# Feature-first copies of x, memory and norms, and one pinned order for the first loads

## The chip, the cores and the metric

The kernel runs on one NeuronCore of a Trainium2 chip. A core has five engines with an instruction stream each: TensorE (PE, matmuls and transposes; PEld is its weight load, which overlaps), VectorE (DVE), ScalarE (ACT), GpSimd (POOL) and SyncE (SP, here only the issuer of loads). Each works in the order in which its instructions stand and waits on semaphores. Sixteen DMA engines carry out the transfers that SP, ACT and POOL issue. The metric is the time of one execution in microseconds, lower is better. The kernel before took 2638.45 us, the median of three timed runs.

## The reference

Four layers on a sequence of 256 tokens of width 2048, in float32. Every layer norms x, makes one combined input projection, runs a mixer (latent attention, sparse attention, sliding window, latent attention), adds four heads of cross-attention to a memory of 256 tokens, gates the lot and projects it back:

```
mem_n = rmsnorm(mem, mem_norm)
for i in range(4):
    h = rmsnorm(x, norm_in[i])
    self_out, mq, gate = mixer(h, w_in)          # by layer: MLA, DSA, SWA, MLA
    mem_out = memory_attention(mq, mem_n @ w_mem_kv[i])
    y = concat(self_out, mem_out) * silu(gate)
    x = x + y @ w_out[i]
return rmsnorm(x, final_norm)
```

For this change two facts matter. A product `rmsnorm(m, g) @ w` contracts over the 2048 features, so TensorE wants the features of m on the partitions, each multiplied by its g; the factor 1/rms of a row can be applied to the result. And all four `mem_n @ w_mem_kv[i]` depend on memory alone.

## The kernel before, in words

Precision first: a float32 operand is split into a high and a low part (`split`: ACT copies the high part to the fast matmul type at L60, DVE subtracts it at L64), and a product is three matmuls, high by high, high by low and low by high. Every weight therefore passes through ACT (`wh`) and DVE (`wl`), three buffers each, after its load into one of five buffers `wr` of 512 KB (`stage`, L207, on SP's queue).

`rows_by` (L234 to L236) computes a 256 x 512 product with tokens as rows: per k-tile of 128 features six matmuls, and two k-tiles per load. `columns_by` (L253, L257) computes one with features as rows, in the same way.

The program begins with `memory()`. It loads memory in rows, in four tiles `mrow` of 512 features, on SP's and ACT's queues; loads the norm weights as rows and transposes them into `gvec` (`vectors_T`, L91); transposes each memory tile with TensorE, multiplies it by its norm weights and splits it (`to_features`, L186 to L188); and sums the squares of the rows on ACT (`square_sum`, L197) for 1/rms, `mrstd` by rows and `mbc` spread over columns. The result `mT` feeds eight equal steps (two for each layer): a `rows_by` product for two heads' values, `acc_mv`, scaled by `mrstd` as it leaves PSUM, and two `columns_by` products for two heads' keys, `acc_mk`, scaled by `mbc`. POOL writes them to HBM (`mv`, `mkT`) for later.

Within the first step stand also `late_constants` (x by rows in four loads of 512 KB at L115, three norm vectors, masks, rotary tables) and, at its end, the same transposing and splitting for x (`Norm.chunk`, into `xT`) with its sums and 1/rms (`Norm.finish`), and the bias tables (`bias_table`, `pt` at L142). After each step one table copy of 1.5 MB goes out on POOL's queue (`tab<-flat`, L151), after the second step two. `mrow`, the keys on their way out and later tiles share five buffers, `pq`.

The order on each engine is set by a scheduler that moves instructions by modelled times; only what is passed through `keep_in_program_order` keeps its place. Loads of SP and ACT share eight semaphores in turn, so at most eight are in flight, and one more waits for the landing of an older one.

Of the kernel before, what the change touches and what calls it, by code (L numbers as in the profile page):

```python
# [8 lines left out]
F32 = mybir.dt.float32  # L9
# [22 lines left out]
def kernel(ctx: ExitStack, tc: tile.TileContext, a: dict, out: bass.AP,  # L32
# [10 lines left out]
    def misc(name, dt=F32):  # L43
        return ps.tile([P, 512], dt, name=name, tag="mp", bufs=4)
# [27 lines left out]
    rows = cst.tile([P, P], F32, name="rows")  # L72
    mrow = []

    def vectors(src, o, n, eng):
        if len(src.shape) == 2:
            src = src.rearrange("l d -> (l d)")
        eng.dma_start(rows[o:o + n, :], src.rearrange("(r c) -> r c", c=P))

    def memory_rows(c):  # L80
        q = act.tile([P, 2, 512], F32, name="mrow", tag="pq", bufs=PQ)
        mrow.append(q)
        for t in range(2):
            eng = nc.scalar if t else nc.sync
            eng.dma_start(q[:, t, :], min_[t][:, c * 512:(c + 1) * 512])

    gvec = cst.tile([P, P], F32, name="gvec")

    def vectors_T(o, n):
        gp = misc("gp")  # L90
        nc.tensor.transpose(gp[:, :n], rows[o:o + n, :], ident[o:o + n, o:o + n])  # L91
        nc.vector.tensor_copy(gvec[:, o:o + n], gp[:, :n])
# [9 lines left out]
    nc.vector.tensor_copy(identr, ident)  # L102
    ones = cst.tile([P, P], F32, name="ones")
    nc.vector.memset(ones, 1.0)

# [2 lines left out]
    sin = cst.tile([P, 2, A_ROPE], F32, name="sin")  # L108
    nsink = cst.tile([P, 32], F32, name="nsink")

    def late_constants():
        for c in range(2):
            for t in range(2):
# [13 lines left out]
        nc.vector.tensor_scalar(nsink, nsink, -1.0, None, op0=OP.mult)  # L127
# [54 lines left out]
    def to_features(dst, t, src, gcol, n=4):  # L182

        tp = misc("tp")
        for j in range(n):
            nc.tensor.transpose(tp[:, j * P:(j + 1) * P], src[:, j * P:(j + 1) * P], ident)  # L186
        xg = tmp("xg")
        nc.vector.tensor_mul(xg[:, :n * P].rearrange("p (j c) -> p j c", j=n),  # L188
                             tp[:, :n * P].rearrange("p (j c) -> p j c", j=n),
                             gvec[:, gcol:gcol + n][:, :, None].to_broadcast([P, n, P]))  # L190
        sl = slice(t * P, (t + 1) * P)
        g3 = xg[:, :n * P].rearrange("p (j c) -> p j c", j=n)
        split(dst[:, 0, :n, sl], dst[:, 1, :n, sl], g3)

    def square_sum(col, src):
        junk = tmp("junk")
        nc.scalar.activation(junk[:, :src.shape[-1]], src, AF.Square, accum_out=col)  # L197
# [21 lines left out]
        split(wh[:, :n], wl[:, :n], wr[:, c0:c0 + n])  # L219
        return wh, wl  # L220

    def rows_by(xt, kts, w, k0, cols, name):

        acc = [ps.tile([P, 512], F32, name=f"acc_{name}{t}", tag="acc", bufs=4) for t in range(2)]
        for s in range(0, kts, ST):
            m = min(ST, kts - s)
            wr, n = stage(w, k0 + s, m, cols)
            for k in range(m):
                wh, wl = parts_of(wr, k * n, n)
                q = xt[(s + k) // 4]  # L230
                for t in range(2):
                    xh, xl = (q[:, v, (s + k) % 4, t * P:(t + 1) * P] for v in range(2))
                    first, last = s + k == 0, s + k == kts - 1
                    nc.tensor.matmul(acc[t][:, :n], xh, wh[:, :n], start=first, stop=False)  # L234
                    nc.tensor.matmul(acc[t][:, :n], xh, wl[:, :n], start=False, stop=False)  # L235
                    nc.tensor.matmul(acc[t][:, :n], xl, wh[:, :n], start=False, stop=last)  # L236
        return acc
# [38 lines left out]
    class Norm:  # L276
# [32 lines left out]
    def memory():  # L309
        mrstd = cst.tile([P, 2], F32, name="mrstd")  # L310
        m16 = cst.tile([P, 2], F32, name="m16")
        mbc = act.tile([P, S], F32, name="mbc", tag="kr", bufs=1)
        mss = small("mss", 8, bufs=2)
        mT = []
        for c in range(4):
            if c < 2:
                memory_rows(c + 2)
            q = act.tile([P, 2, 4, S], F32R, name="mT", tag=f"big{c}")
            mT.append(q)
            for t in range(2):  # L320
                to_features(q, t, mrow[c][:, t, :], c * 4)
                square_sum(mss[:, t * 4 + c:t * 4 + c + 1], mrow[c][:, t, :])
        s2 = small("ms2", 2)
        nc.vector.tensor_reduce(s2, mss.rearrange("p (t c) -> p t c", t=2), AX.X, OP.add)
        rsqrt_mean(mrstd, s2, D)
        nc.vector.tensor_scalar(m16, mrstd, 0.0625, None, op0=OP.mult)
        spread(mbc, m16)
        copies = [(v, g) for v in range(2) for g in range(4)]
        for i in range(depth):
            w = a["w_mem_kv"][i]  # L330
            for p_ in range(2):
                acc = rows_by(mT, 16, w, 0, (MEMW + p_ * 512, 512), "mv")
                v = [act.tile([P, 2, 512], F32R, name="mv", tag="aux", bufs=AUX) for z in range(2)]
                for t in range(2):
                    sc = mrstd[:, t:t + 1]
                    copy_act(v[0][:, t, :], acc[t], scale=sc)
                    nc.vector.scalar_tensor_tensor(v[1][:, t, :], acc[t], sc, f32(v[0])[:, t, :],
                                                   op0=OP.mult, op1=OP.subtract)
                for z in range(2):
                    nc.gpsimd.dma_start(mv[i][p_][:, z], v[z])  # L340
                if i == p_ == 0:
                    late_constants()
                for h in (2 * p_, 2 * p_ + 1):
                    acc = columns_by(mT, 16, w, 0, (h * 256, 256), "mk")
                    kT = act.tile([P, 2, 2, S], F32R, name="mkT", tag="pq", bufs=PQ)
                    for j in range(2):
                        z = total(acc[j])
                        zs = wk.tile([P, S], F32, name="zs", tag="z", bufs=3)
                        nc.vector.tensor_mul(zs, z, mbc)
                        split(kT[:, 0, j, :], kT[:, 1, j, :], zs)  # L350
                    nc.gpsimd.dma_start(mkT[i][h], kT)
                step = 2 * i + p_
                if step == 0:
                    for c in range(4):
# [500 lines left out]
def _constants():  # L855
# [18 lines left out]
            "c_cos": np.concatenate([c, c], 1), "c_sin": np.concatenate([-s, s], 1)}  # L874


_INS = ["x", "mem", "norm_in", "final_norm", "mem_norm", "rel_bias", "w_in_a", "a_q_norm", "w_uq",
        "a_kv_norm", "w_ukv", "w_in_b", "w_in_c", "c_sinks", "w_mem_kv", "w_out"]


# [19 lines left out]
```

## Time and profile before

| | |
|---|---|
| timed runs | 2636.72, 2638.45, 2638.67 us (median 2638.45) |
| profiled execution | 2637.23 us, span 2635.0 us |
| busy | PE 2605.1 us (99%), DVE 1890.2 (72%), ACT 1625.5 (62%), POOL 57.8 (2%) |
| first matmul of the first product | 13.84 us after the span's start |
| memory's eight steps | until about 376 us |
| moved by DMA | 507.50 MB, mean 193 GB/s; 262 to 290 GB/s in the first 400 us |

A row of the timeline gives start and duration in us, engine, line, operation, tiles, shape and count, and in brackets the idle time before it with its cause. A row of windows gives the stretch and its length, then busy time (and instructions) of PE, PEld, DVE, ACT and POOL, the granted TensorE clock, the share of the DMA engines and GB/s; restricted to a tile, engines without such instructions are left out. A row of DMA issues ends with the median time from issue to landing. A row of groups gives the total and mean (ns) time and the idle time in front. A row of the chain gives start, duration and what it was. A row of waits gives total, times and longest.

### The profile page before, as it was taken

How to read it: one execution, taken by the hardware profiler on the slowest of the kernel's cores; microseconds unless marked ns; L12 is line 12 of the kernel's file. 1: busy time of each engine (PE TensorE's matmuls, PEld its weight loads, DVE VectorE, ACT ScalarE, POOL GpSimd, SP SyncE). 2: the span in 40 equal slices, each digit the busy share in tenths (PEclk: the TensorE clock that was granted, in tenths of full speed). 3: DMA queues.
4: the chain of work that ended last, by engine and by line, in shares of the span. 5: the costliest groups of instructions: out<-in, count | busy, mean ns of one | idle time of the engine just before them, and what ended most of it. 6: DMA issues, size and time to landing. Idle time of an engine off the chain costs nothing.

```text
span 2635.0 us, 43048 instructions
## 1 busy us (share of the span) xinstructions
PE 2605.1 (99%) x14623; PEld 2260.1 (86%) x14623; DVE 1890.2 (72%) x4174; ACT 1625.5 (62%) x3460; POOL 57.8 (2%) x102
## 2 busy tenths in 40 slices
PE   8999999999999999999999999999999999999998
PEld 7888888888888889888888888888888888888886
DVE  7566656677767685877777776777778767776767
ACT  6455556556656566666666666676666655665655
POOL 1000000000000000000000000000000000000000
PEclk9999999999999999999999999999999999999999
DMA  7898886666557666565556665555555766665764
GB/s 268 272 290 275 273 265 199 165 187 168 169 160 224 192 189 171 167 183 170 175 164 190 188 191 176 173 172 177 191 168 162 206 163 188 165 171 156 226 183 135
DMA packets 454064, 507.50 MB, mean 193 GB/s; under 512 B 69300, under 2 KB 352180, under 8 KB 452692
## 3 DMA queue, kind: packets, MB, share of 16 engines
q1 hardware_dynamic: 439716, 446.42, 57.3%
q0 software_dynamic: 13120, 56.17, 6.7%
q8 instruction: 115, 1.88, 0.3%
q10 hardware_dynamic: 1008, 2.16, 0.2%
q14 instruction: 105, 0.86, 0.1%
HBM read 485.70 MB, written 31.56 MB: 196 GB/s over the span
## 4 chain that ended last, share of the span: by engine, by line
PE 97%; DMA 1%; DVE 1%; ACT 0%; issue 0%; ACTq 0%; POOLq 0%
PE acc_g L253 14%; PE acc_g L257 7%; PE acc_wo L234 7%; PE acc_wo L235 7%; PE acc_wo L236 7%; PE acc_mq L253 5%; PE acc_mk L253 5%; PE acc_qn L253 3%; PE acc_cq L253 3%; PE acc_mq L257 2%; PE acc_mk L257 2%; PE acc_q L234 2%; PE acc_q L235 2%; PE acc_q L236 2%; PE acc_mv L235 2%; PE acc_mv L236 2%
## 5 line engine op out<-in xcount | busy, mean ns | idle before, releaser
L64 DVE TENSOR_TENSOR wl<-wr,wh 128x512 fp32r<-128x512 f32 (+2 forms) x1776 | 1172.9, 663 | 642.9 <-ACT wh L60 612.7
L60 ACT ACTIVATE wh<-wr 128x512 fp32r<-128x512 f32 (+2 forms) x1776 | 1079.9, 609 | 846.1 <-PE acc_g L253 186.0
L253 PE MATMUL acc_g<-xT,wh 128*128 128x512 f32 x1536 | 488.9, 397 | 0.6 <-DVE z L264 0.6
L257 PEld LDWEIGHTS acc_g<-xT,wl 128*128 128x128 f32 x1536 | 285.2, 188 | 60.7
L257 PE MATMUL acc_g<-xT,wl 128*128 128x256 f32 x1536 | 311.0, 280 | 0.0
L235 PE MATMUL acc_wo<-wl,y 128*128 128x512 f32 x768 | 302.5, 394 | 0.6 <-DVE wl L64 0.5
L236 PE MATMUL acc_wo<-wh,y 128*128 128x512 f32 x768 | 299.1, 390 | 0.0
L253 PEld LDWEIGHTS acc_g<-xT,wh 128*128 128x128 f32 x1536 | 238.1, 189 | 4.7 <-issue 1.1
L234 PE MATMUL acc_wo<-wh,y 128*128 128x512 f32 x768 | 240.4, 393 | 0.7 <-ACT wh L60 0.6
L235 PEld LDWEIGHTS acc_wo<-wl,y 128*128 128x128 f32 x768 | 144.3, 188 | 30.0 <-DVE wl L64 1.4
L236 PEld LDWEIGHTS acc_wo<-wh,y 128*128 128x128 f32 x768 | 144.2, 188 | 28.4
L234 PEld LDWEIGHTS acc_wo<-wh,y 128*128 128x128 f32 x768 | 141.3, 188 | 27.8 <-ACT wh L60 1.0
L253 PE MATMUL acc_mk<-mT,wh 128*128 128x512 f32 x512 | 160.8, 396 | 1.4 <-ACT wh L60 1.4
L253 PE MATMUL acc_mq<-xT,wh 128*128 128x512 f32 x512 | 161.7, 397 | 0.0
L807 DVE TENSOR_TENSOR x<-x,acc_wo 128x512 f32<-128x512 f32 x192 | 125.5, 681 | 7.2 <-PE acc_wo L236 6.9
L253 PE MATMUL acc_qn<-cT,wh 128*128 128x512 f32 x384 | 123.2, 399 | 0.0
L253 PE MATMUL acc_cq<-xT,wh 128*128 128x512 f32 x384 | 120.8, 396 | 0.0
L257 PEld LDWEIGHTS acc_mk<-mT,wl 128*128 128x128 f32 x512 | 95.8, 188 | 22.7 <-DVE wl L64 0.4
L257 PEld LDWEIGHTS acc_mq<-xT,wl 128*128 128x128 f32 x512 | 93.7, 188 | 20.0
L257 PE MATMUL acc_mq<-xT,wl 128*128 128x256 f32 x512 | 102.5, 281 | 0.0
L235 PE MATMUL acc_q<-wl,xT 128*128 128x512 f32 x256 | 102.4, 400 | 0.0
L257 PE MATMUL acc_mk<-mT,wl 128*128 128x256 f32 x512 | 100.8, 278 | 0.0
(284 smaller groups left out, 4453.5 us busy)
## 6 DMA issues: line engine op xcount, KB each, us to landing
wr<-in_w_out_dram SPq DMA_DIRECT2D x192, 512.0 KB, 3.7
wr<-in_w_in_a_dram SPq DMA_DIRECT2D x176, 512.0 KB, 4.2
wr<-in_w_mem_kv_dram SPq DMA_DIRECT2D x128, 512.0 KB, 5.2
wr<-in_w_in_b_dram SPq DMA_DIRECT2D x112, 512.0 KB, 3.7
wr<-in_w_in_c_dram SPq DMA_DIRECT2D x104, 512.0 KB, 3.7
wr<-in_w_uq_dram SPq DMA_DIRECT2D x288, 128.0 KB, 2.8
tab<-flat POOLq DMA_DIRECT2D x8, 1536.0 KB, 10.9
wr<-in_w_in_a_dram SPq DMA_DIRECT2D x32, 288.0 KB, 3.0
```

Source lines behind the costliest of these rows:

```text
L60: nc.scalar.activation(o, i, AF.Copy, scale=scale)
L64: nc.vector.tensor_sub(lo, src, f32(hi))
L234: nc.tensor.matmul(acc[t][:, :n], xh, wh[:, :n], start=first, stop=False)
L235: nc.tensor.matmul(acc[t][:, :n], xh, wl[:, :n], start=False, stop=False)
L236: nc.tensor.matmul(acc[t][:, :n], xl, wh[:, :n], start=False, stop=last)
L253: nc.tensor.matmul(acc[j], wh[:, o:o + P], q[:, :, kt % 4, :], start=kt == 0, stop=False)
L257: nc.tensor.matmul(acc[j][:, 0, :], wl[:, o:o + P], q[:, 0, kt % 4, :], start=False, stop=kt == kts - 1)
L807: nc.vector.tensor_add(xs, xs, acc[t])
```

## The change

x, memory and the norm weights come in a second layout, features on partitions (`l_x`, `l_mem`: 128 x 16 x 256; `l_norms`: all weights as columns of one 128 x 128 tile), made before the launch. `gvec` is loaded whole. A tile `ft` of features is multiplied and split straight from its load, in parts 256 wide: ACT writes the high part with the norm weight as scale, DVE the low one (`weighted_parts`). The transposes of memory, of x for layer 0 and of the norm rows go; those of x between layers stay.

All loads of the first step go on SP's queue in one pinned order: norms, first features, and then features between weights. Memory and x are still read by rows as well, for the sums of squares and the residual: memory's rows behind the first product's weights, x's rows behind the weights of steps 2 to 5 (steps counted from 0), a quarter each. A quarter of x's features follows each, and `finish` moves to step 6. The first values leave PSUM after the first key head, behind the row scales.

```diff
+    gvec = cst.tile([P, P], F32, name="gvec")
+    tc.keep_in_program_order(nc.sync.dma_start(gvec, a["l_norms"]))
+
+    def features(src, c):
+        q = act.tile([P, 4, S], F32, name="ft", tag="pq", bufs=PQ)
+        for k in range(0, 4, 2):
+            tc.keep_in_program_order(
+                nc.sync.dma_start(q[:, k:k + 2, :], src[:, 4 * c + k:4 * c + k + 2, :]))
+        return q
+
+    mft = [features(a["l_mem"], 0)]
     ident = cst.tile([P, P], F32, name="ident")
-    nc.scalar.dma_start(ident, a["c_ident"])
...
-    memory_rows(0)
-    vectors(a["mem_norm"], 0, 16, nc.gpsimd)
-    memory_rows(1)
-    vectors_T(0, 16)
...
+    def first_rows(c):
+        for t in range(2):
+            cs = slice(c * 512, (c + 1) * 512)
+            tc.keep_in_program_order(nc.sync.dma_start(x[t][:, cs], xin[t][:, cs]))
+
     def late_constants():
-        for c in range(2):
-            for t in range(2):
-                cs = slice(c * 1024, (c + 1) * 1024)
-                nc.sync.dma_start(x[t][:, cs], xin[t][:, cs])
-        vectors(a["norm_in"], 64, 64, nc.sync)
-        vectors(a["a_q_norm"], 32, 24, nc.sync)
-        vectors(a["a_kv_norm"], 56, 8, nc.sync)
-        vectors_T(64, 64)
-        vectors_T(32, 32)
...
+    def weighted_parts(dst, src, gcol):
+        for k in range(4):
+            g = gvec[:, gcol + k:gcol + k + 1]
+            copy_act(dst[:, 0, k, :], src[:, k, :], scale=g)
+            nc.vector.scalar_tensor_tensor(dst[:, 1, k, :], src[:, k, :], g, f32(dst)[:, 0, k, :],
+                                           op0=OP.mult, op1=OP.subtract)
...
-    def rows_by(xt, kts, w, k0, cols, name):
+    def rows_by(xt, kts, w, k0, cols, name, prepare=None):
...
             wr, n = stage(w, k0 + s, m, cols)
+            if prepare is not None and s % 4 == 0:
+                prepare(s // 4)
...
+            if self.layer == 0:
+                weighted_parts(q, features(a["l_x"], c), 64 + c * 4)
             for t in range(2):
                 src = x[t][:, c * 512:(c + 1) * 512]
-                to_features(q, t, src, 64 + self.layer * 16 + c * 4)
+                if self.layer:
+                    to_features(q, t, src, 64 + self.layer * 16 + c * 4)
                 square_sum(self.ss[:, t * 4 + c:t * 4 + c + 1], src)
...
+        def prepare(c):
+            if c < 3:
+                mft.append(features(a["l_mem"], c + 1))
+            if c == 1:
+                tc.keep_in_program_order(nc.sync.dma_start(ident, a["c_ident"]))
+                nc.vector.tensor_copy(identr, ident)
+            weighted_parts(mT[c], mft[c], c * 4)
...
+                begins = i == p_ == 0
+                acc = rows_by(mT, 16, w, 0, (MEMW + p_ * 512, 512), "mv", prepare if begins else None)
+                if begins:
+                    mrow = [memory_rows(c) for c in range(4)]
+                else:
+                    values(i, p_, acc)
+                for h in (2 * p_, 2 * p_ + 1):
+                    acck = columns_by(mT, 16, w, 0, (h * 256, 256), "mk")
+                    if begins and h == 0:
+                        row_scales(mrow)
+                        values(i, p_, acc)
+                    keys(i, h, acck)
+                if begins:
                     late_constants()
...
                 if step == 0:
-                    for c in range(4):
-                        nm.chunk(c)
-                    nm.finish()
                     bias_table(0)
                     bias_table(1)
+                if 2 <= step < 6:
+                    first_rows(step - 2)
+                    nm.chunk(step - 2)
+                if step == 6:
+                    nm.finish()
```

`values`, `keys` and `row_scales` hold the code that stood in the loop and ahead of it before.

More of the change, by code (lines that the diff above doesn't have):

```diff
@@ L101 @@
     identr = cst.tile([P, P], F32R, name="identr")
-    nc.vector.tensor_copy(identr, ident)
     ones = cst.tile([P, P], F32, name="ones")
@@ L313, in memory @@
         mss = small("mss", 8, bufs=2)
-        mT = []
-        for c in range(4):
[L316 to L319, printed above, removed]
-            for t in range(2):
[L321 to L324, printed above, removed]
@@ L325, in memory @@
-        rsqrt_mean(mrstd, s2, D)
-        nc.vector.tensor_scalar(m16, mrstd, 0.0625, None, op0=OP.mult)
-        spread(mbc, m16)
+        mT = [act.tile([P, 2, 4, S], F32R, name="mT", tag=f"big{c}") for c in range(4)]
+        def prepare(c):
[5 more added lines that the diff above has]
+            weighted_parts(mT[c], mft[c], c * 4)
@@ new lines, in memory_rows, with row_scales @@
+        def memory_rows(c):
+            q = act.tile([P, 2, 512], F32, name="mrow", tag="pq", bufs=PQ)
+            for t in range(2):
+                tc.keep_in_program_order(
+                    nc.sync.dma_start(q[:, t, :], min_[t][:, c * 512:(c + 1) * 512]))
+            return q
+        def row_scales(mrow):
+            for c in range(4):
+                for t in range(2):
+                    square_sum(mss[:, t * 4 + c:t * 4 + c + 1], mrow[c][:, t, :])
+            s2 = small("ms2", 2)
+            nc.vector.tensor_reduce(s2, mss.rearrange("p (t c) -> p t c", t=2), AX.X, OP.add)
+            rsqrt_mean(mrstd, s2, D)
+            nc.vector.tensor_scalar(m16, mrstd, 0.0625, None, op0=OP.mult)
+            spread(mbc, m16)
@@ new lines, in values @@
+        def values(i, p_, acc):
+            v = [act.tile([P, 2, 512], F32R, name="mv", tag="aux", bufs=AUX) for z in range(2)]
+            for t in range(2):
+                sc = mrstd[:, t:t + 1]
+                copy_act(v[0][:, t, :], acc[t], scale=sc)
+                nc.vector.scalar_tensor_tensor(v[1][:, t, :], acc[t], sc, f32(v[0])[:, t, :],
+                                               op0=OP.mult, op1=OP.subtract)
+            for z in range(2):
+                nc.gpsimd.dma_start(mv[i][p_][:, z], v[z])
@@ L328, in memory, with keys @@
+        def keys(i, h, acc):
+            kT = act.tile([P, 2, 2, S], F32R, name="mkT", tag="pq", bufs=PQ)
+            for j in range(2):
+                z = total(acc[j])
+                zs = wk.tile([P, S], F32, name="zs", tag="z", bufs=3)
+                nc.vector.tensor_mul(zs, z, mbc)
+                split(kT[:, 0, j, :], kT[:, 1, j, :], zs)
+            nc.gpsimd.dma_start(mkT[i][h], kT)
         copies = [(v, g) for v in range(2) for g in range(4)]
@@ L889 @@
     arrays, args = {}, {}
-    for name, v in [(n, inputs[n]) for n in _INS] + list(_constants().items()):
+    for name, v in ([(n, inputs[n]) for n in _INS] + list(_laid_out(inputs).items())
+                    + list(_constants().items())):
         v = _np.ascontiguousarray(v)
```

50 lines of the change are left out of this document (11 added, 39 removed).

## The prediction

> **What bounds the kernel now.** I read the page's busy shares first, then the first microseconds instruction by instruction, then TensorE's waits, then stretches by window, then the loads' times to landing.
>
> ```profile
> span 2635.0 us, 43048 instructions
> PE 2605.1 (99%) x14623; PEld 2260.1 (86%) x14623; DVE 1890.2 (72%) x4174; ACT 1625.5 (62%) x3460; POOL 57.8 (2%) x102
> ...
> PE gp L91 <- DMA rows<-in_mem_norm_dram: 7.2, 1, 7.2
> PE acc_kvb L234 <- ACT wh L60: 1.8, 1, 1.8
> PE acc_mk L253 <- ACT wh L60: 1.4, 1, 1.4
> ...
> 200.00:250.00 50.00, 50.00 (x253) 42.39 (x252) 32.07 (x56) 27.49 (x50) 3.46 (x7) 1.00 0.84 264
> ```
>
> PE is busy 99% of the span, and 50.00 of 50 us in a stretch of the memory stage. It waits 7.2 us for the first load and hardly at all later. So whatever leaves PE's order shortens the time, and whatever makes PE wait lengthens it. Nothing else counts. The start, row by row:
>
> ```profile
> 7.15 0.28 PE L91 MATMUL gp<-ident,rows 16*128 16x16 f32 x1 [7.15 <-DMA rows<-in_mem_norm_dram]
> 7.37 4.71 PE L186 MATMUL tp<-ident,mrow 128*128 128x128 f32 x28
> 13.84 0.73 PE L234 MATMUL acc_mv<-wh,mT 128*128 128x512 f32 x2 [0.67 <-ACT wh L60]
> 15.73 0.42 PEld L234 LDWEIGHTS acc_mv<-wh,mT 128*128 128x128 f32 x2
> 22.67 0.41 PEld L234 LDWEIGHTS acc_mv<-wh,mT 128*128 128x128 f32 x2
> 25.39 0.41 PEld L234 LDWEIGHTS acc_mv<-wh,mT 128*128 128x128 f32 x2
> ...
> 35.39 1.09 PE tp L186 x10
> ```
>
> The real matmuls begin at 13.84. One k-tile of `rows_by` (six matmuls) takes 1.36 us (22.67 to 25.39 is two). The second k-tile begins at 15.73, so the stream runs as if it had begun at 15.73 - 1.36 = 14.37 us. Ten transposes of x take 1.09 us, 0.109 each.
>
> **The change, part by part.** The built order of PE is the old one without 67 instructions: 32 transposes of memory, 32 of x, 3 of the norm rows. A few `spr` and `pt` matmuls stand elsewhere; the rest keeps its order to the end.
>
> *Transposes of x and norms.* The 32 of x lie inside packed PE time (the first step): 32 x 0.109 = -3.5 us. Of the three `gp`, two lie there, about 0.15 each: -0.3.
>
> *The start.* The new order on SP's queue is norms (64 KB), first memory features (512 KB), first weights (512 KB), features, two weights, features, `ident`, two weights, features, weights. No POOL load is in the way any more. What moved in the first microseconds (last column, GB/s), and two landings:
>
> ```profile
> 0.00:2.00 2.00, 0.00 (x0) 0.00 (x0) 0.23 (x2) 0.00 (x0) 0.93 (x6) 1.00 0.11 14
> 2.00:4.00 2.00, 0.00 (x0) 0.00 (x0) 0.00 (x0) 1.49 (x2) 0.42 (x1) 1.00 0.84 235
> 4.00:6.00 2.00, 0.00 (x0) 0.00 (x0) 0.23 (x1) 0.72 (x2) 0.00 (x0) 1.00 0.75 214
> 6.00:8.00 2.00, 0.85 (x4) 0.81 (x5) 0.17 (x1) 0.00 (x0) 0.00 (x0) 1.00 1.02 382
> 8.00:10.00 2.00, 2.00 (x12) 2.00 (x11) 1.32 (x3) 0.76 (x2) 0.00 (x0) 1.00 1.02 367
> 12.00:14.00 2.00, 0.89 (x6) 0.58 (x6) 2.00 (x4) 2.00 (x6) 0.00 (x0) 1.00 1.05 404
> ...
> mrow<-in_mem_dram SPq DMA_DIRECT2D x1, 256.0 KB, 3.7
> wr<-in_w_mem_kv_dram SPq DMA_DIRECT2D x1, 512.0 KB, 7.9
> ...
> L60 ACT ACTIVATE wh<-wr 128x512 fp32r<-128x512 f32 x256 | 160.7, 631 | 152.2 <-PE acc_mk L253 65.6 <-DVE wl L64 50.4 <-PE acc_mv L236 24.4
> L60 ACT ACTIVATE mkT<-zs 128x256 fp32r<-128x256 f32 x32 | 13.2, 412 | 4.4 <-DVE zs L349 4.4
> L64 DVE TENSOR_TENSOR wl<-wr,wh 128x512 fp32r<-128x512 f32 x256 | 175.8, 690 | 121.5 <-ACT wh L60 119.4
> L349 DVE TENSOR_TENSOR zs<-z,mbc 128x256 f32<-128x256 f32 x32 | 13.5, 421 | 0.5
> L197 ACT ACTIVATE junk<-mrow 128x512 f32<-128x512 f32 x8 | 4.9, 617 | 0.8 <-DMA mrow<-in_mem_dram 0.8
> L197 ACT ACTIVATION_READ_ACCUMULATOR junk<-mrow 128x1 f32 x8 | 1.5, 186 | 0.0
> ```
>
> Summed, 0.50 MB have moved by 4 us, 0.93 by 6, 1.69 by 8, 2.42 by 10, about 3.2 by 12 and 4.0 by 14. The first weights were issued at 4.64 with 2.1 MB ahead of them and landed 7.9 us later, at 12.55. The curve has their last byte at about 10.7, so a landing shows some 1.8 us after the last byte; the very first load showed less, near 1. Read off the same curve: first features (0.59 MB) at 4.4, landed about 5.8; first weights (1.11 MB) 6.5, landed 8.1; third features (3.21 MB) 12.1, landed 13.8. (I take 1.4 to 1.7.) ACT makes four 256-wide parts (0.41 each, the `mkT` row) from 5.8 to 7.4 and the first `wh` (0.63) from 8.1, so the first matmul starts near 8.75 instead of 13.84.
>
> That is not the gain. In ACT's new order the four parts of the third features stand ahead of the `wh` of k-tile 4, and ACT waits in order: 13.8 + 4 x 0.41 + 0.63 = 16.1. PE's k-tile 4 begins there, as if the stream had begun at 16.1 - 4 x 1.36 = 10.65. DVE's `wl` (0.69) comes behind and costs 0.2 more. Gain 14.37 - 10.65 - 0.2 = **3.5 us**. Bounds: 5.3 (the old gain in first matmul, 5.1, and the 0.2), and nothing (if the curve of one queue alone lies 3 us lower).
>
> PE's own first matmuls have to be done by 16.1 too, and may be slow:
>
> ```profile
> 7.30:10.30 3.00, 2.94 (x14) 2.94 (x15) 1.38 (x2) 1.00 1.05 378
> 10.30:12.40 2.10, 1.77 (x16) 1.53 (x14) 1.31 (x2) 1.00 1.02 375
> ...
> 390.00:392.60 2.60, 0.80 (x6) 0.57 (x5) 0.26 (x1) 0.73 (x2) 0.00 (x0) 1.00 1.09 381
> 392.60:396.00 3.40, 3.40 (x15) 3.21 (x15) 1.49 (x4) 1.27 (x4) 0.00 (x0) 0.51 0.66 197
> ```
>
> By the first two rows (transposes alone) 14 transposes fit into 3.0 us up to 10.3, and 16 into 1.8 us after: PE ran at half pace for its first 3.2 us, though the clock column reads 1.00. By the last two, the clock fell to 0.51 for 3.4 us behind the 1.8 us wait of `acc_kvb`. Before, the half pace fell on transposes; now it falls on matmuls. 3.4 us at half pace lose 1.7 us: four k-tiles from 8.75 end at 8.75 + 5.44 + 1.7 = 15.9, just covered by the 16.1. [...]
>
> *Square sums of memory.* The rows now arrive behind the first eight weights, and the eight squares (0.617 + 0.186 = 0.80 each) stand between the `wh` of k-tiles 11 to 16. With three `wh` buffers ACT leads PE by 2 x 1.36 - 0.65 = 2.07 us. Two squares and a `wh` per k-tile cost 2.23 against 1.36, so the lead falls to 1.2, 0.3, then -0.6 at the third. The two single squares add 0.1: PE waits **+0.7**. Bounds: 0, and +3 (rows landing later than their 24 to 28 us by the same curve). The value evacuation waits for this chain now, behind six `wh` of the next product; PSUM's four buffers cover it until the second key head.
>
> *Constants.* `ident` moves from ACT's queue to SP's. The one-hot and mask loads on POOL follow the square sums, whose buffers they share. Of the two `pt`, the first moves forward to about 40 us; the one-hot lands by about 36 (issued near 30, about 5 us as before). Nothing on PE; if that cover went, PE would wait in order.
>
> *x rows and x features.* The rows (2 MB) leave the first step and go, 512 KB each, behind the last weights of steps 2 to 5. Features of x (2 MB more, and as much for memory) go behind the sixth weights of steps 3 to 6, pinned in SP's queue. Weight issues there wait for buffers, and land well ahead:
>
> ```profile
> wr<-in_w_mem_kv_dram SPq DMA_DIRECT2D x1, 512.0 KB, 4.3
> ...
> wr<-in_w_mem_kv_dram SPq DMA_DIRECT2D x1, 512.0 KB, 10.8
> ...
> 155.86 8.82 SPq L207 DMA_DIRECT2D wr<-in_w_mem_kv_dram  x4
> 160.27 0.63 ACT L60 ACTIVATE wh<-wr 128x512 fp32r<-128x512 f32 x1
> 160.93 0.69 DVE L64 TENSOR_TENSOR wl<-wr,wh 128x512 fp32r<-128x512 f32 x1
> 161.60 0.53 POOL L151 DMA_DIRECT2D tab<-flat  x1
> 162.28 0.69 DVE L64 TENSOR_TENSOR wl<-wr,wh 128x512 fp32r<-128x512 f32 x1 [0.66 <-ACT wh L60]
> 164.09 0.61 PE L234 MATMUL acc_mv<-wh,mT 128*128 128x512 f32 x2
> ```
>
> The first row is the sixth weights of step 3, issued at 155.86; the second are weights issued at 249.76, as a table copy starts. The features go out at about 156.3 and land near 161.3, just before the table copy of 161.60. ACT's four parts stand behind the `wh` of 160.27: they run 161.3 to 162.9, the next `wh` ends at 163.6, DVE's last part at 163.4 and its `wl` at 164.3. PE needs that `wl` two matmuls after 164.09, at 164.54. A margin of 0.2 us: I take 0.15 lost per chunk, four chunks, **+0.6**; bounds 0, and the late case below. ACT's squares of x (1.6 us a step) have a whole step of slack.
>
> **Sum:** -3.5 - 3.5 - 0.3 + 0.7 + 0.6 = -6.0 us. The profiled execution took 2637.23 (span 2635.0), 1.2 under the median 2638.45. Over it and the three timed ones (2636.72, 2638.45, 2638.67) the mean is 2637.8, and 2637.8 - 6.0 = **2631.8 us**. A change under 0.2%, 5.3 us, can't be told from none here; so faster means below 2633.2.
>
> **The rivals.**
>
> [...] Chance 0.21.
>
> *A better start.* The third features land 1.8 us sooner (400 GB/s from 3 us on), the waits vanish: -5.3 - 3.8 = -9.1, 2628.7. Against it: the slow first rows. Chance 0.13.
>
> *Features of x late (slower).* If they fall into the table copy, they land like the weights of 249.76, 10.8 us after issue instead of about 5: 5.8 more, 0.2 of it covered. PE waits 5.6 in each of steps 3 to 6: -6.6 + 22.4 = +15.8, 2653.6, and 1.7 more for each fall of the clock. It is slower from waits of 11.9 in all (6.6 + 5.3), 3 us a chunk: landing 8 us after issue. For it: the copy starts 0.3 us behind the expected landing, and SP, ACT and DVE all wait in order. Against it: the features are queued 5 us before it, and the row beside them landed in 4.3. Chance 0.10.
>
> *The forecast* has 0.56. About a seventh of it (0.08) lies above 2633.2.
>
> **How the numbers follow.** Faster: 0.48 + 0.13 = 0.61. Same: 0.08 + 0.21 = 0.29. Slower: 0.10. The range runs from 2627.5 (below the better start) to 2637.5 (no gain at the start and 2 us of waits more); the slow case and small tails are left out.
>
> **What would show it.** The first matmul near 8.75 us and steady k-tiles as if from about 10.7; no `tp` from memory or x; ACT waiting for `ft` ahead of k-tile 4; a PE wait under 1 us at k-tiles 14 to 16; waits under 0.5 us after the x features in steps 3 to 6; the waits of `acc_mk` (1.4) and `acc_kvb` (1.8) kept. It is wrong if PE waits for `wh` or `wl` in steps 3 to 6 by microseconds, if loads take longer from one queue, or if later stages shift.

## The result and the profile after

The changed kernel took 2635.20 us (median of 22 runs, 2631.20 to 2638.32); the kernel before took 2638.26 (22 runs, 2635.82 to 2640.70). The ratio is 0.9988, 95% interval 0.9983 to 0.9994: 3.1 us less, clear of no change, but inside the 0.2% that the prediction called "same". The profiled execution took 2636.80 us with a span of 2634.7, against 2637.23 and 2635.0, so in the two traces only 0.3 us is left between them (the traced run of before was 1.0 us under its median, that of the changed kernel 1.6 over). They show how that small number comes about: 7.9 us were won in the first 100 us, and 7.6 were lost again before 405 us.

The first part of the page and the view of TensorE's waits, after (waited for: us in total, times, longest):

```profile
span 2634.7 us, 42943 instructions
...
PE 2601.2 (99%) x14556; PEld 2254.7 (86%) x14556; DVE 1884.1 (72%) x4171; ACT 1628.8 (62%) x3476; POOL 57.3 (2%) x101
```

```profile
PE acc_mv L227 <- ACT wh L60: 10.0, 2, 8.7
PE acc_kvb L227 <- ACT wh L60: 3.1, 1, 3.1
PE acc_mk L246 <- ACT wh L60: 2.4, 1, 2.4
```

PE has 67 instructions fewer and 3.9 us less to do, as the built order said. But the two waits that the prediction kept, 1.4 us for `acc_mk` and 1.8 for `acc_kvb`, are now 2.4 and 3.1, and `acc_mv` has a new one of 1.3 beside the 8.7 of the start.

Reading off both traces when PE begins each product gives the lead of the changed kernel place by place (steps counted from 0, as in the prediction; from `acc_cq` to the end PE's order is the same in both):

| PE begins | before | after | lead |
|---|---|---|---|
| step 2, values | 109.90 | 102.00 | 7.90 |
| step 3, values | 155.90 | 150.57 | 5.33 |
| step 4, values | 199.97 | 194.62 | 5.35 |
| step 5, values | 244.02 | 239.26 | 4.76 |
| step 6, values | 288.08 | 283.96 | 4.12 |
| step 6, keys | 309.85 | 307.62 | 2.23 |
| layer 0, `acc_kva` | 376.18 | 374.44 | 1.74 |
| layer 0, `acc_cq` | 405.20 | 404.86 | 0.34 |

**The start.** The timeline of after (start us, us, engine, line, operation, tiles; in brackets the idle time before and what ended it), and then stretches of it by window (length, then PE, PEld, DVE, ACT and POOL busy with the number of instructions, granted clock, DMA share, GB/s):

```profile
4.41 1.88 ACT L60 ACTIVATE mT<-ft,gvec 128x256 fp32r<-128x256 f32 x4 [2.17 <-DMA ft<-in_l_mem_dram]
...
8.05 1.15 ACT L60 ACTIVATE wh<-wr 128x512 fp32r<-128x512 f32 x2 [1.76 <-DMA wr<-in_w_mem_kv_dram]
...
8.73 1.22 PE L227 MATMUL acc_mv<-wh,mT 128*128 128x512 f32 x2 [8.73 <-ACT wh L60]
...
12.81 1.71 ACT L60 ACTIVATE mT<-ft,gvec 128x256 fp32r<-128x256 f32 x4 [0.49 <-DMA ft<-in_l_mem_dram]
...
14.42 0.62 ACT L60 ACTIVATE wh<-wr 128x512 fp32r<-128x512 f32 x1
...
16.95 0.62 PE L227 MATMUL acc_mv<-wh,mT 128*128 128x512 f32 x2
```

```profile
11.46:14.43 2.97, 2.97 (x8) 2.31 (x7) 2.50 (x7) 2.25 (x6) 0.00 (x0) 1.00 1.05 379
14.43:16.95 2.52, 2.52 (x13) 2.07 (x11) 1.83 (x4) 1.24 (x3) 0.00 (x0) 1.00 1.05 387
...
127.07:130.48 3.41, 3.41 (x12) 2.99 (x12) 3.10 (x5) 2.08 (x4) 1.09 (x2) 0.50 1.05 339
```

The first matmul stands at 8.73. The third features came at 12.81, a microsecond sooner than expected, and the weights of k-tile 4 were ready by 15.04. But PE reached k-tile 4 only at 16.95: until 14.43 it was never idle and did 8 matmuls in 2.97 us, after it 13 in 2.52. Half pace lasted 5.7 us, from 8.73 to 14.43.

ACT's squares of memory's rows stand two to a `wh` (timeline of after). The last row is the seventh k-tile of the kernel before, with which it reached its steady pace (timeline of before):

```profile
25.71 0.62 ACT L60 ACTIVATE wh<-wr 128x512 fp32r<-128x512 f32 x1
26.23 0.62 ACT L187 ACTIVATE junk<-mrow 128x512 f32<-128x512 f32 x1
26.85 0.62 ACT L187 ACTIVATE junk<-mrow 128x512 f32<-128x512 f32 x1
27.46 0.62 ACT L60 ACTIVATE wh<-wr 128x512 fp32r<-128x512 f32 x1
...
22.89 0.61 PE L234 MATMUL acc_mv<-wh,mT 128*128 128x512 f32 x2
```

**The double table copy.** The timeline of after around the two table copies of step 1, and the DMA queues from 113 to 121 us (q1 carries SP's loads, q0 POOL's; packets, MB, share of the 16 engines' time; the last line is an issue, its size and us to landing):

```profile
107.69 1.06 POOL L133 DMA_DIRECT2D tab<-flat  x2
...
119.36 1.17 ACT L60 ACTIVATE wh<-wr 128x512 fp32r<-128x512 f32 x2 [1.55 <-DMA wr<-in_w_mem_kv_dram]
...
125.70 1.15 ACT L60 ACTIVATE wh<-wr 128x512 fp32r<-128x512 f32 x2 [5.17 <-DMA wr<-in_w_mem_kv_dram]
...
126.38 0.73 PE L246 MATMUL acc_mk<-mT,wh 128*128 128x512 f32 x2 [2.44 <-ACT wh L60]
```

```profile
q0 software_dynamic: 223, 2.52, 90.9%
q1 hardware_dynamic: 179, 0.19, 10.2%
...
wr<-in_w_mem_kv_dram SPq DMA_DIRECT2D x3, 512.0 KB, 12.8
```

The same place in the timeline of before:

```profile
115.58 1.06 POOL L151 DMA_DIRECT2D tab<-flat  x2
...
132.53 1.15 ACT L60 ACTIVATE wh<-wr 128x512 fp32r<-128x512 f32 x2 [4.12 <-DMA wr<-in_w_mem_kv_dram]
```

In the 8 us from 113 to 121 of after the weights got 0.19 MB, 24 KB a microsecond, and landed 12.8 us after their issue. The two queues sent about as many packets, 223 and 179, but the copy's hold 11 KB each and the weights' 1, so the bytes divided 13 to 1. PE waited 2.4 us here, and the clock then ran at half for 3.41 us (the row of 127.07 above); before it waited 1.4, and the clock stayed at 1.00 (133.2 to 140.0).

**The features of x.** The timeline of after in step 6:

```profile
284.38 0.96 SPq L80 DMA_DIRECT2D ft<-in_l_x_dram  x2
...
289.66 0.53 POOL L133 DMA_DIRECT2D tab<-flat  x1
...
291.29 1.71 ACT L60 ACTIVATE xT<-ft,gvec 128x256 fp32r<-128x256 f32 x4 [2.33 <-DMA ft<-in_l_x_dram]
...
292.90 1.66 ACT L60 ACTIVATE wh<-wr 128x512 fp32r<-128x512 f32 x3
...
293.57 0.73 PE L227 MATMUL acc_mv<-wh,mT 128*128 128x512 f32 x2 [1.26 <-ACT wh L60]
```

Features issued at 284.4 landed 6.9 us later, and ACT stood 2.33 us before them. The three `wh` behind them then ran without a gap, so their weights had been there: the order on ACT made PE wait, not the weights.

**The stored keys and values.** The DMA queues of after from 379 to 389 us, where the products `acc_kva` and `acc_kvb` run:

```profile
q0 software_dynamic: 546, 2.01, 64.8%
q1 hardware_dynamic: 812, 0.89, 30.4%
...
wr<-in_w_in_a_dram SPq DMA_DIRECT2D x6, 288.0 KB, 8.2
mkr<-mkT POOLq DMA_DIRECT2D x1, 512.0 KB, 10.2
```

POOL's reads of the stored keys and values for the first attention part take two thirds of the DMA time, and weights land after 8.2 us. Before, in the same stretch, it was 56% and 6.6 us, and the wait was 1.8 us instead of 3.1. The weights for which `acc_kvb` waited, before and after (timelines):

```profile
391.87 0.78 ACT L60 ACTIVATE wh<-wr 128x288 fp32r<-128x288 f32 x2 [2.21 <-DMA wr<-in_w_in_a_dram]
...
391.43 1.27 ACT L60 ACTIVATE wh<-wr 128x288 fp32r<-128x288 f32 x3 [3.52 <-DMA wr<-in_w_in_a_dram]
```

### The profile page after: what moved, and what is told of

Its sections match the earlier page's. It is cut to its first block, busy times and chain, and to the rows that moved or that the text cites. A ratio compares the mean times of both kernels' runs of the same rounds, so it can differ in the third digit from the quotient of the medians.

```text
span 2634.7 us, 42943 instructions
## 1 busy us (share of the span) xinstructions
PE 2601.2 (99%) x14556; PEld 2254.7 (86%) x14556; DVE 1884.1 (72%) x4171; ACT 1628.8 (62%) x3476; POOL 57.3 (2%) x101
## 4 chain that ended last, share of the span: by engine, by line
PE 97%; DMA 1%; DVE 1%; ACT 0%; issue 0%; SPq 0%; ACTq 0%
PE acc_g L246 14%; PE acc_g L250 7%; PE acc_wo L227 7%; PE acc_wo L228 7%; PE acc_wo L229 7%; PE acc_mq L246 5%; PE acc_mk L246 5%; PE acc_qn L246 3%; PE acc_cq L246 3%; PE acc_mq L250 2%; PE acc_mk L250 2%; PE acc_q L227 2%; PE acc_q L228 2%; PE acc_q L229 2%; PE acc_mv L227 2%; PE acc_mv L228 2%
```

## The experiments

Two theories stood against each other for what gave the gain back. S, starved weights: the table copies leave the weights too little, so a PE that runs ahead only waits longer there. L, added loads: the 4 MB of rows and features that the change puts behind the first weights crowd the weights out. All ratios are to the kernel before, timed in the same rounds on the same chip; each ratio is followed by its 95% interval. Waits of PE are its idle time, as the view of waits gives it.

**a_memory.** Memory by features, x by rows and turned on PE in step 0, as before.

```diff
-            if self.layer == 0:
-                weighted_parts(q, features(a["l_x"], c), 64 + c * 4)
...
-                if self.layer:
-                    to_features(q, t, src, 64 + self.layer * 16 + c * 4)
+                to_features(q, t, src, 64 + self.layer * 16 + c * 4)
```

> The memory half alone: features of memory as in the changed kernel, x by rows and transposed in the first step as before. Two theories of where the gain of 7.9 us (changed kernel, at the start of the third step) went. S, starved weights: the table copies hold the DMA engines, and whatever PE gains ahead of them is partly lost in longer waits there. L, added loads: the 4 MB of extra rows and features crowd out the weights. Both: first matmul at 8.7 us, third step begins about 4.5 us earlier than before (7.9 less the 3.5 of the x transposes). S: 2 to 3 us of that are given back at the double table copy after the second step, though no x load is left there; the time ends 1.5 to 3 us under before. L: the wait at the double copy stays at before's 1.5 us, the whole 4.5 us are kept.

2637.65 us, ratio 0.9999 (0.9991 to 1.0008). The first matmul stood at 8.94, but PE waited 2.1 us at the end of the first product, where seven squares of memory's rows stood in a row on ACT ahead of the next `wh`, which then waited 0.6 us more for its weights (start of the last square, then of that `wh`, then PE):

```profile
33.14 0.61 ACT L186 ACTIVATE junk<-mrow 128x512 f32<-128x512 f32 x1
...
34.41 1.15 ACT L60 ACTIVATE wh<-wr 128x512 fp32r<-128x512 f32 x2 [0.57 <-DMA wr<-in_w_mem_kv_dram]
...
35.09 0.73 PE L245 MATMUL acc_mk<-mT,wh 128*128 128x512 f32 x2 [2.13 <-ACT wh L60]
```

Its lead at step 2 was 1.6 us, where 4.5 had been expected, and the double copy (1.8 us of wait, with a half clock behind it) took that away.

**b_x.** x by features, memory by rows.

```diff
-        for c in range(2):
-            for t in range(2):
-                cs = slice(c * 1024, (c + 1) * 1024)
-                nc.sync.dma_start(x[t][:, cs], xin[t][:, cs])
...
+            if self.layer == 0:
+                weighted_parts(q, features(a["l_x"], c), 64 + c * 4)
```

> The x half alone: memory by rows and transposed as before; rows and features of x in steps 2 to 5 as in the changed kernel. Both theories: first matmul at 13.8 us as before, third step begins 3.5 us earlier (32 transposes of 0.109). S: a wait of 1.5 to 2.6 us at the double copy, as with the memory half alone, and about 1.4 us in step 6, where x features and a table copy follow each other; the time ends 0 to 3 us under before. L: waits grow in each of steps 3 to 6, and the time ends at before's or over it.

2638.37 us, 1.0000 (0.9991 to 1.0009). The lead at step 2 was 3.0, close to the 3.5 of the transposes. The double copy took 2.5 of it (wait 2.4, half clock), and steps 3 to 6, with features as late as in the changed kernel, a further 2.9. So the half that adds most loads lost in both places. Neither half alone pays.

**c_warm.** The changed kernel, with 36 matmuls of ones on PE before the first real one.

```diff
+    wm = misc("wm")
+    for z in range(36):
+        tc.keep_in_program_order(nc.tensor.matmul(wm[:, :P], ones, ones, start=True, stop=True))
```

> The changed kernel and 36 matmuls of a tile of ones by itself on PE ahead of the first weights (results unused), so that PE is busy from about 1.1 us. The changed kernel ran its first three k-tiles at half pace until 14.4 us and began k-tile 4 at 16.95 us; ACT had its high part ready at 15.04. If the pace bound the start: k-tile 4 begins at 15.1 us, 1.9 us sooner, all k-tiles at 1.36 us. If the loads bound it: no change at k-tile 4. At the end S lets 0 to 2 us of it through.

2637.78 us, 0.9995 (0.9986 to 1.0004). I had sized it wrongly: the 36 kept PE until 10.7 us, 2 us past the point where the weights were ready, so it can't tell pace from loads; full pace came at 4.43, and PE then waited 1.1 us at 20.9 for a `wh` that stood behind late features. It is repeated below with 26.

**d_small.** The changed kernel, with the copied table's rows padded, so that a copy goes out in smaller packets.

```diff
-                      ap=[[0, P], [1, 8 * N_TAB]])
-        tc.keep_in_program_order(nc.gpsimd.dma_start(tabs[v][g].rearrange("p h n -> p (h n)"), src))
+                      ap=[[0, P], [N_TAB, 8], [1, N_TAB]])
+        tc.keep_in_program_order(nc.gpsimd.dma_start(tabs[v][g][:, :, :N_TAB], src))
```

> The changed kernel with the table copies in rows of 1.5 KB (the tables' rows are padded to 400 elements) where the trace has packets of 12 KB; the same bytes. S, with packets served in turn: the weights get a good half of the engines during a copy and land in 5 to 8 us instead of 9 to 16; the waits of 2.6 us (and the half pace of 3.4 us behind it) at the double copy and 1.4 us in step 6 go, the wait at acc_kvb (3.1 us, behind reads of keys and values) stays: 4 to 6 us faster than the changed kernel, near 2630. L: no change, since the same loads are there. A third outcome: 1024 rows a copy cost POOL or the engines more, and the copies take longer than a step.

2635.73 us, 0.9990 (0.9981 to 0.9999): not told apart from the changed kernel, where theory S had expected 4 to 6 us. The packets, 4.4 KB instead of 11.3, gave the weights twice the bytes in the same stretch (113 to 121 us):

```profile
q0 software_dynamic: 503, 2.20, 82.7%
q1 hardware_dynamic: 349, 0.37, 17.9%
...
wr<-in_w_mem_kv_dram SPq DMA_DIRECT2D x3, 512.0 KB, 11.5
```

The wait there fell from 2.4 to 1.3 us, no half clock followed, and the lead at step 3 was 7.3 instead of 5.3. Then waits of 1.3 us came in steps 4 and 6, which lost 1.9 us each, and `acc_kvb` waited 3.1. So S holds for its place, and something else is at work later.

**h_late, i_before_late.** All eight copies out of the memory stage: each is issued on ACT's queue where an attention part of the first two layers begins. The first has this edit on the changed kernel, the second on the kernel before.

```diff
-                for c in copies[:2 if step == 1 else 1]:
-                    table_copies(*c)
-                copies = copies[2 if step == 1 else 1:]
...
-                y = mixer.attend(*mixer.project(part))
+                pr = mixer.project(part)
+                if i < 2:
+                    table_copies(i, part)
+                y = mixer.attend(*pr)
```

> The changed kernel with the eight table copies taken out of the memory stage: each is issued on ACT's queue as an attention part of the first two layers begins (tables are first read at 830 us). If the copies starve the weights and so give the gain back (theory S): the waits of 2.6 us at the first double copy, the half clock behind it (1.7) and the 1.4 us wait of step 6 go; the third step's first product starts 7.9 us ahead of before's 109.90 as in the changed kernel, and the lead is still some 7.5 at the first product of layer 0 (376.2 before, so 368.7). Only the wait of acc_kvb stays (3.1 against 1.8 before). About -6.5 us, 2631.8, ratio 0.9975. If the added 4 MB of x rows and features crowd the weights out (theory L): waits of 1 to 3 us appear in steps 2 to 6 behind those loads, the lead at 376 is 2 to 4 as in the changed kernel, and the time stays at 2634 to 2635.5, ratio 0.9985 to 0.999. New waits in the attention parts are possible in both; there is slack of DMA there (0.55 to 0.69 busy), I expect none above 0.5 us.

> The kernel before with the same late table copies, as a control. Theory S: its 1.55 us wait at 131 goes and nothing else, -1.5 us, 2636.7, ratio 0.9994; so late copies are worth 1.5 to the kernel before and 3 to 5 to the changed one. Theory L: the same or less; the two theories part only in the comparison with the changed kernel with late copies.

With the change 2633.71 us, 0.9984 (0.9976 to 0.9993); without it 2635.68, 0.9989 (0.9980 to 0.9998). The queues of h_late from 113 to 121 us:

```profile
q1 hardware_dynamic: 1578, 1.57, 60.2%
...
wr<-in_w_mem_kv_dram SPq DMA_DIRECT2D x3, 512.0 KB, 3.5
```

Weights land after 3.5 us, and the wait and the half clock at 127 are gone. The time lies between what the two theories had expected (2631.8, and 2634 to 2635.5). At step 3 the lead is 9.4 us instead of 5.3; the kernel before gains 1.7 by the same edit, and against this control the lead is 7.7. Of the 2.4 more than 5.3, 0.5 was there at step 2 already, so the copies took about 2 us of the gain at that one place. But between step 3 and the keys of step 6 the lead then falls from 9.4 to 3.4, which S did not expect, where i_before_late stays 1.7 throughout. The timeline of ACT in step 4 of h_late:

```profile
199.05 1.71 ACT L60 ACTIVATE xT<-ft,gvec 128x256 fp32r<-128x256 f32 x4 [2.79 <-DMA ft<-in_l_x_dram]
200.66 1.66 ACT L60 ACTIVATE wh<-wr 128x512 fp32r<-128x512 f32 x3
```

It is the picture of step 6 of the changed kernel, now with no table copy in flight: ACT waits 2.8 us for features, ahead of weights that are there (PE then waits 1.7). In steps 3 to 6 it waited four times, 6.5 us in all; and for x's rows, whose squares also stand ahead of `wh`, another 4.6 (PE waited 1.1 for that at 275).

**j_squares_late.** h_late, with the sums of squares taken from the features, so that memory's rows are not loaded at all and x's only behind 40 loads of layer 0.

```diff
+    def feature_squares(sq, src, first):
+        for k in range(0, 4, 2):
+            part = src[:, k:k + 2, :].rearrange("p a b -> p (a b)")
...
+                tc.keep_in_program_order(nc.scalar.activation(junk, part, AF.Square))
+                nc.vector.tensor_add(sq, sq, junk)
...
-                if begins:
-                    mrow = [memory_rows(c) for c in range(4)]
```

> The changed kernel with late copies and without the rows in the memory stage: the sums of squares of memory and x are taken from the features (ACT squares on two 512-wide pieces a chunk, DVE adds, and four matmuls against a column of ones), memory's rows are never loaded and x's rows (2 MB) are loaded behind 40 loads of layer 0's first products. So the memory stage carries 4 MB less. Theory S: as the changed kernel with late copies, 2631 to 2632.5. Theory L: only here the waits of steps 2 to 6 go, 2631 to 2632 against 2634 to 2635 there. Either way the wait of acc_kvb stays near 2 to 3 us, since the reads of the stored keys and values stand there. The added squares may cost PE up to 0.7 us in step 0.

2631.28 us, 0.9973 (0.9963 to 0.9982). The features stand at the same places in the order and landed a median of 4.4 us after their issue (h_late 6.0, the changed kernel 5.5); ACT waited for them once, 0.9 us. The lead falls from 9.2 at step 3 to 6.9 at step 6's keys, 2.3 instead of 6.1, though two waits of 0.5 for `wl`, behind the added squares, cost PE some 0.8 each. So the part of L that lies in steps 3 to 6 holds: without the rows and their squares there the features came in time. The two went together, so this run doesn't tell the rows' bytes from the squares that wait for them. `acc_kvb` still waited 3.1.

**k_late_warm.** h_late with 26 matmuls of ones first (the edit of c_warm, with 26).

> The changed kernel with late copies and 26 matmuls of ones before the first real one (36 lasted until 10.7 us; 26 should end near 8.6). It tells what set the start: if PE's half pace held k-tile 4 (16.95 instead of 16.1), the first product of the second step comes 0.8 to 1.3 us earlier than with late copies alone; if loads set it, within 0.3 us of it, with a PE wait of about 1 us for the fourth features before 21 us.

2631.44 us, 0.9974 (0.9965 to 0.9983). Full pace came at 4.35, the first real matmul at 8.58, and step 1 began at 56.33 instead of 57.71: 1.4 us sooner. So PE's pace had set the start, not the loads. They stand close behind it: at full pace ACT waited 0.9 us for the third features (k_late_warm, 12.6 us).

**l_pinned, n_all.** k_late_warm with the x parts pinned on ACT behind eight more weights, which meant pinning the `wh` copies of steps 2 to 6 too; n_all has the reads of the next experiment as well.

```diff
+    def copy_pinned(o, i, scale=1.0):
+        z = nc.scalar.activation(o, i, AF.Copy, scale=scale)
+        if pin[0]:
+            tc.keep_in_program_order(z)
...
+                if 3 <= 2 * i + p_ < 7:
+                    nm.chunk(2 * i + p_ - 3)
...
-                    nm.chunk(step - 2)
+                    nm.ft.append(features(a["l_x"], step - 2))
```

> The changed kernel with late copies and 26 warm-up matmuls, and the four feature parts of x pinned on ACT behind eight more weights (from the 51st load's to the 56th's), with their loads a load earlier: some 22 us between issue and use instead of 5 to 6. Theory F (the features come late, and ACT waits for them in order, ahead of weights already there): the waits of 0.5, 2.2, 1.0 and 0.3 us at 152, 198, 244 and 290 go, -3.9 us against 2631.4, 2627.5. Theory L (the bytes crowd the weights, whatever the order): waits of the same sum come back a few us later as weights that land late, 2630.5 to 2631.5. The pins also put pieces of the stored keys side by side on ACT; that may cost PE 0.3 us a head at most.

> Both of these: late copies, 26 warm-up matmuls, x's feature parts pinned later, reads of stored keys and values later. If all four causes are what they seem, no PE wait above 0.5 us is left in the first 400 us, -3.9 and -4.5 against 2631.4: 2623, ratio 0.994. If bytes are the limit, 2627 or more.

2688.48 us, 1.0191 (1.0177 to 1.0205), and 2685.90, 1.0182 (1.0168 to 1.0196). A miss by construction. The evacuations of keys, which had stood between the `wh` copies, now stood in one block between two products, and ACT waited in it for PE, for DVE and for x's rows. One such place in l_pinned:

```profile
135.56 0.63 ACT L197 ACTIVATE junk<-x 128x512 f32<-128x512 f32 x1 [2.88 <-DMA x<-in_x_dram]
...
139.97 0.73 PE L257 MATMUL acc_mk<-mT,wh 128*128 128x512 f32 x2 [3.56 <-ACT wh L65]
```

In 16 such waits for `wh` PE lost 38 us. Whether features issued earlier would end the late features is left open.

**m_reads, o_before_all.** The first reads of stored keys and values taken from POOL and issued on ACT's queue behind the products of the first memory queries: m_reads on k_late_warm, o_before_all on i_before_late.

```diff
+        if behind:
+            for z in range(2):
+                tc.keep_in_program_order(nc.scalar.dma_start(f32(kT[z]), f32(mkT[i][2 * part + z])))
+            for z in range(2):
+                tc.keep_in_program_order(nc.scalar.dma_start(f32(v[z]), f32(mv[i][part][:, z])))
```

> The changed kernel with late copies and 26 warm-up matmuls, and the four reads of the first stored keys and values (2 MB) taken from POOL at 368 to 381 us and issued on ACT's queue behind the products of the first memory queries. If these reads starve the weights of the first products of layer 0, the wait of acc_kvb (3.1) falls below 0.5 and the half clock behind it (3.4 us, 1.7 lost) goes: -4.5 us against 2631.4, 2627. If that wait comes from the products' own weights, it stays near 3 and the time near 2631.4.

> The kernel before with the same late copies and late reads, as control: its 2.4 us wait of acc_kvb and the half clock behind it go, -4 us against 2635.7: 2631.7. What is then left between this and the kernel with all four is the change itself without its crowding: -6.0 as predicted, and 1 to 2 of the warm start.

2628.34 us, 0.9960 (0.9948 to 0.9973), the fastest of all; and 2631.16, 0.9974 (0.9964 to 0.9985). The queues of m_reads from 379 to 389 us:

```profile
q1 hardware_dynamic: 1844, 2.00, 70.9%
q0 software_dynamic: 77, 0.25, 8.8%
...
wr<-in_w_in_a_dram SPq DMA_DIRECT2D x6, 288.0 KB, 3.2
```

Weights land after 3.2 us instead of 8.2, and neither kernel waits at `acc_kvb`. The reads were the cause. In m_reads the features of x took the gain instead: its lead, 11.7 at step 3, was 4.4 at `acc_kva`, with waits of 0.8 and 1.6 us and this half clock behind the second (windows of m_reads):

```profile
287.45:290.87 3.42, 1.83 (x8) 0.99 (x7) 3.26 (x7) 2.86 (x7) 0.00 (x0) 1.00 0.63 225
290.87:294.28 3.41, 3.41 (x10) 2.67 (x9) 1.01 (x2) 0.87 (x2) 0.00 (x0) 0.50 0.57 183
```

So with copies and reads out of the way, the change and a warm start together are worth 2.8 us by medians (2631.16 to 2628.34) and 2.3 by spans (2629.3 and 2627.0). They were timed in the same rounds, and all five runs of m_reads (2625.84 to 2629.04) lie below all eight of o_before_all (2630.97 to 2631.34). That is far from the 7 to 8 expected: 7.3 us of the lead of 11.7 were lost again in steps 3 to 7, where ACT waited 6.5 us for features of x and 4.2 for its rows. Whether the edit of j_squares_late would keep the lead there was not run. Moving the copies and reads alone, with nothing else changed, was worth more: 6.9.

## Why the prediction was right or wrong

2631.8 was forecast, with a range of 2627.5 to 2637.5 and 0.61 on "faster"; 2635.2 lies in the range, but of the 6.0 us forecast 3.1 came, and that is "same" by the prediction's own bound, which had 0.29.

- *Start, -3.5.* The first matmul came as worked out (8.75 forecast, 8.73 found), and the weights of k-tile 4 were ready a microsecond sooner (16.1 forecast, 15.04 found). But PE reached k-tile 4 only at 16.95, and steady k-tiles ran as if from 16.95 - 4 x 1.36 = 11.5, not 10.65. Before, they ran as if from 22.89 - 6 x 1.36 = 14.7: the 14.37 was read off a weight load, 0.23 us ahead of its matmul, and PE lost another 0.1 behind it. So the start gave 3.2 us. That this is close to 3.5 is luck: the loads alone would have let k-tile 4 begin at 15.04, 1.9 us sooner. The step that failed is "PE ran at half pace for its first 3.2 us": taken from before, where PE began at 7.15, it was 5.7 us for a PE that began at 8.73. k_late_warm, at full pace from 4.35, shows that this was the limit, and not the loads: its step 1 began 1.4 us sooner.
- *Transposes, -3.5, and norm rows, -0.3.* These held. Between the two traces 7.9 us lie up to step 2; 3.2 are the start, 0.5 four `spr` matmuls that only moved to step 7 (and are paid there), and the other 4.2 are these, against 3.8. Single transposes between products cost little more than the 0.109 of ten in a row: with 14 of them the two key heads of step 0 took 23.95 us, without any they take 22.28, so 0.12 each.
- *Square sums, +0.7.* Nothing was lost in the changed kernel: from k-tile 4 to the end of the first product PE took 33.27 - 16.95 = 16.3 us, 12 k-tiles of 1.36. The squares did stand two to a `wh`, as forecast, but the term was mis-sized: from one `wh` to the next took 27.46 - 25.71 = 1.75 us, not 2.23, because the durations that the prediction added overlap (a square and its read begin 0.61 us before the next instruction, not 0.80). Three times 0.39 over the pace of 1.36 stays inside the lead of 2.07. In a_memory, where seven stood together, PE waited 2.1, within the bound of 3.
- *x features, +0.6.* The term that was most wrong, inside the forecast's own mechanism: 0.0, 0.6, 0.6 and 1.9 us in steps 3 to 6, 3.1 in all. "Land near 161.3", 5 us after issue, was near the median (5.5), but the last chunk took 7.0, and ACT waits for the slowest. The rival "features of x late" named the mechanism (ACT waits in order, ahead of weights); its cause, the table copy, is not needed: h_late has it without any copy. "ACT's squares of x have a whole step of slack" was wrong as well: they waited for their rows three times, 3.2 us in all, though PE lost at most 0.2 to that here (1.1 at once in h_late).
- *Waits kept.* "The waits of `acc_mk` (1.4) and `acc_kvb` (1.8) kept" was the step that failed outright. The first became 2.4, with a half clock behind it that before had not: 1.1 and 1.5 us, 2.6 of lead lost. The second grew by 1.3. I had treated them as fixed prices; they are ends of queues. The copies and reads were issued as much sooner as PE came, but the weights behind them landed by less: at the double copy ACT had them 6.8 us sooner (125.70 against 132.53) for a PE that came 7.9 sooner, at `acc_kvb` 0.4 sooner (391.43 against 391.87) for a PE that came 1.7 sooner. Why the transfers then took longer is not shown. h_late takes the first of these waits away, m_reads both.

The sum of the traces: 7.9 won; 2.6 lost at the double copy, 3.1 at x's features, 0.5 at the moved `spr`, 1.4 at `acc_kvb`; 0.3 left. The median of the runs kept 3.1. The runs spread from 2631 to 2638 us; which of these waits the median one escapes was not seen, since each kernel has one trace. Part of the spread goes with the clock: the six runs with a mean granted clock of 0.998 averaged 2633.7 us, the fifteen with 0.997 2635.2.

## What to carry to other kernels

Work taken off the bounding engine early is only a loan until the next place where a transfer, not that engine, sets the time: list every wait behind the edit, ask what its releaser waits for, and count the gain only up to the first one whose landing does not move as far. When a bulk copy shares the DMA engines with a stream of small packets, move it to a stage with slack before tuning anything else; here that was worth 2.5 us to the kernel before, and with the reads 6.9, more than the change. And what stands in an in-order queue ahead of ready work needs a margin by the slowest landing seen, not the median.

## What the runs showed of the hardware

Packets were shared far more evenly than bytes (223 to 179 in the changed kernel, 503 to 349 in d_small): at 11.3 KB against 1.06 KB a packet the weights got 24 KB/us, at 4.4 KB 46, and without the copy 196 (113 to 121 us in each, and in the last PE did not ask for more).

The clock fell to half behind some waits and not behind others. In the first 400 us it fell to 0.50 for 3.41 us behind waits of 2.4 and 3.1 us in the changed kernel (from 127.07 and 393.31), of 1.8 in the kernel before (from 392.64) and of 1.6 in m_reads (from 290.87). It stayed at full behind 1.4 us in the kernel before (ended at 133.2), 1.3 in step 6 of the changed kernel (ended at 293.57), 1.7 in step 4 of h_late, and 2.7 in h_late (387 to 390). So 1.6 us were enough once and 2.7 were not, and one wait can be worth 1.7 us, half of 3.41, more than another of its length. What else decides is not settled.

The half pace of the start did not last equally long either. PE reached full pace 3.2 us after its first instruction in the kernel before (7.15 to 10.35), 5.7 in the changed kernel (8.73 to 14.43), 3.3 in k_late_warm and c_warm (1.09 to 4.35 and 4.43), and, with nearly the same start as the changed kernel, 4.3 in a_memory (8.94 to 13.22) and 6.1 in j_squares_late (8.25 to 14.35). What sets it is not shown. By an estimate from these last two, half of the 1.8 us between them, the start can differ by 0.9 us from one execution to the next.
